# Score products of two heads: row halves instead of a stacked high and low part, in a one-layer encoder trunk

## The chip, the cores and the metric

The kernel runs on one core of one Trainium2 chip. The time is that of the device for one execution, in microseconds (us). An execution under the profiler gives the trace from which all rows below are taken; its busy times, waits and clocks belong to that one execution.

## The reference, cut to what matters

The input x has 2048 positions of 1024 values. One layer has two groups of attention heads beside each other, then an output projection, then a gated feed-forward block with a short convolution, and a last norm.

```
h = rmsnorm(x, attn_norm_g)
qa, ka, va, qb, kb, vb = split(h @ w_in, 6)          # 512 columns each
# group a: 8 heads of 64, each query chunk of 64 sees its own and the 8 chunks before it
scores = q k^T / 8 + relative bias;  o = softmax(scores) @ v
# group b: 4 heads, each with two score maps of width 64, all earlier chunks
w = softmax(q1 k1^T / 8 + bias) - lam * softmax(q2 k2^T / 8 + bias);  o = rmsnorm(w @ v)
x = x + concat(oa, ob) @ w_out
u = causal_dwconv(rmsnorm(x) @ w_up);  x = x + (silu(gate) * val) @ w_down
return rmsnorm(x)
```

What the change touches are the products q k^T of both groups. A score map contracts over 64 values. Two maps are always computed together: two heads of group a, or the two maps of one head of group b. The kernel calls them the two heads of a pair, and so does this text.

## The kernel before, in words

Each float32 operand of a product is held as two float16 parts, a high part and a low part (what the high part left over). A product is then three products: high by high, high by low, low by high (TERMS, line 64). The helper split (line 127) makes the parts: ScalarE writes the high part, then VectorE writes source minus high part as the low part.

The program has three stages. From 0 to 93 us x is normalised and transposed and the first projections run. From 93 to 1112 us the attention runs, in eight passes of one head pair each (ORDER, line 442). After that come the output projection, the feed-forward block and the last norm.

A pass holds 16 query blocks of 128 rows. For each, a front makes scores, biases and the softmax (front_a, line 464; front_b, line 526), and a back, two blocks later, multiplies by v (back_a, back_b). A front goes through pieces of 128 to 512 keys. For a piece it takes two score banks in PSUM, one a head, out of a pool of four (ps_s, line 210), calls scores, and lets VectorE add the bias and reduce the maximum (lines 484 and 543); only then is the bank free. Between the pieces stand the projections of the next pass as fill: proj_k makes the keys of 512 positions, proj_q the queries of 256. Their result stands in PSUM with head 0 on partitions 0 to 63 and head 1 on 64 to 127.

Before the change, proj_k splits each head by itself so that head 0's keys lie stacked in one slot, high part on partitions 0 to 63, low part on 64 to 127; head 1's lie the other way round in the second slot. proj_q also splits each head by itself, and two DMAs from ScalarE's queue then copy each head's high part to the other half of the partitions. So one product over 128 rows gives high query by high plus low key at once (line 438), and a product over 64 rows adds low query by high key (line 440).

The order of instructions on each engine is made when the program is built: a scheduler places them by a modelled time line, with the fronts, backs and splits at a raised priority. Each engine then executes its own list in that order and waits by semaphores.

Of the kernel before, what the change touches and what calls it, by code (L numbers as in the profile page):

```python
# [8 lines left out]
F16 = mybir.dt.float16  # L9
# [9 lines left out]
P = 128  # L19
# [29 lines left out]
QS = 2.0 ** -19  # L49
# [14 lines left out]
TERMS = ((0, 0), (0, 1), (1, 0))  # L64
# [3 lines left out]
def kernel(  # L68
# [18 lines left out]
    nc = tc.nc  # L87
# [39 lines left out]
    def split(hi, lo, src, scale):  # L127

        A.activation(hi, src, AF.Copy, scale=scale)  # L129
        V.scalar_tensor_tensor(lo, src, scale, hi, ALU.mult, ALU.subtract)  # L130
# [73 lines left out]
    with ExitStack() as at:  # L204
        kv = at.enter_context(tc.tile_pool(name="kv", bufs=8))
# [165 lines left out]
        def project(ps, hl, h, t0, t1, step):  # L371

            n = 0
            for c in range(NC):
                for a, b in TERMS:
                    nc.tensor.matmul(ps, lhsT=hl[:, a, c, :], rhs=h[:, b, c, t0:t1], start=n == 0, stop=n == 3 * NC - 1)  # L376
                    n += 1
                    if n % step == 0 and n < 3 * NC:
                        yield

        def proj_k(w, tg):

            ps = ps_mm.tile([P, TG], F32, name="mm")
            yield from project(ps, w["hl"][1], hT[tg], 0, TG, 6)
            ks = w["k"][tg] = kv.tile([P, 2, TG], F16, name="ks")
            with tc.high_priority(offset=HP):
                split(ks[0:64, 0], ks[64:128, 0], ps[0:64], QS)
                split(ks[64:128, 1], ks[0:64, 1], ps[64:128], QS)
            yield

        def proj_v(w, tg):
# [25 lines left out]
        def proj_q(w, k):  # L417


            i0 = w["halves"][k] * 2  # L420
            ps = ps_mm.tile([P, 2 * P], F32, name="mq", tag="mm")
            yield from project(ps, w["hl"][0], hT[i0 // 4], i0 % 4 * P, (i0 % 4 + 2) * P, 12)
            qs = w["q"][w["halves"][k]] = kv.tile([P, 2, 2, 2 * P], F16, name="qs", bufs=4)
            with tc.high_priority(offset=HP):
                for hd, (a, b) in enumerate(((0, 64), (64, 128))):
                    split(qs[a:b, hd, 0], qs[a:b, hd, 1], ps[a:b], QS)
            nc.scalar.dma_start(qs[64:128, 0, 0], qs[0:64, 0, 0])
            nc.scalar.dma_start(qs[0:64, 1, 0], qs[64:128, 1, 0])
            yield

        def scores(ps, w, i, k0, k1):


            g = k0 // TG
            ks, kc, qc = w["k"][g], slice(k0 - g * TG, k1 - g * TG), slice(i % 2 * P, (i % 2 + 1) * P)
            qs = w["q"][i // 2]
            for hd in range(2):
                nc.tensor.matmul(ps[hd], lhsT=qs[:, hd, 0, qc], rhs=ks[:, hd, kc], start=True, stop=False)  # L438
            for hd, (a, b) in enumerate(((0, 64), (64, 128))):
                nc.tensor.matmul(ps[hd], lhsT=qs[a:b, hd, 1, qc], rhs=ks[a:b, hd, kc], start=False, stop=True)  # L440

        ORDER = [4, 5, 0, 6, 1, 7, 2, 3]
        oTl = {}
# [20 lines left out]
        def front_a(w, i):  # L464
# [11 lines left out]
            for part, (a, b) in enumerate(((F, W), (0, F))):  # L476
                if a == b:
                    continue
                ps = [ps_s.tile([P, 512], F32, name="s") for hd in range(2)]
                for ka, kb in pieces(k0 + a, k0 + b, ()):  # L480
                    scores([p_[:, ka - k0 - a:kb - k0 - a] for p_ in ps], w, i, ka, kb)
                for hd in range(2):
                    bias = w["far"][:, hd, 384 - F:] if part else w["near"][:, hd, 256 - N:]
                    V.tensor_tensor_reduce(Sm[hd][:, a:b], ps[hd][:, :b - a], bias, 1.0, m[hd],
                                           ALU.add, ALU.max, mx[:, hd, part:part + 1])
                    m[hd] = mx[:, hd, part:part + 1]
                yield
# [38 lines left out]
        def front_b(w, i):  # L526
# [7 lines left out]
            for f, (a, b) in enumerate(reversed(pieces(0, W, (F,)))):  # L534
                ps = [ps_s.tile([P, 512], F32, name="s") for hd in range(2)]
                scores([p_[:, :b - a] for p_ in ps], w, i, a, b)
                for hd in range(2):
                    if a >= F:
                        bias = w["near"][:, hd, 256 - (W - a):256 - (W - b)]
                    else:  # L540
                        bias = w["near"][:, hd, 0:1].to_broadcast([P, b - a])
                    g, a0 = a // 1024, a % 1024
                    V.tensor_tensor_reduce(Sm[hd][g][:, a0:a0 + b - a], ps[hd][:, :b - a], bias, 1.0, m[hd],  # L543
                                           ALU.add, ALU.max, mx[:, hd, f:f + 1])
                    m[hd] = mx[:, hd, f:f + 1]
                yield
# [145 lines left out]
        def weights(n):  # L692

            p = ORDER[n]
            order = list(range(NT)) if p < 4 else [i for a in range(NT // 2) for i in (a, NT - 1 - a)]
            halves = []
            for i in order:
                if i // 2 not in halves:
                    halves.append(i // 2)
            return dict(p=p, order=order, halves=halves, hl={}, E={}, raw={}, k={}, v={}, q={}, P={}, o={}, ssq={})  # L700
# [5 lines left out]
        w = weights(0)  # L706
# [6 lines left out]
        for tg in range(NG):  # L713
            make_h(tg, xts if tg == 0 else None)
            if tg == 0:
                for k, j in enumerate((2, 1, 0)):
                    scan_w(w, ORDER[0], j, raws[k] if k < len(raws) else None)
                    load_w(w, j, (True, KF, Q1)[k])
            proj_v_first(w, tg)
            run(proj_k(w, tg))  # L720
            if tg == 0:
                run(proj_q(w, 0))
                make_lambda()
                make_profiles_b()
                load_bias(w, ORDER[0])
        run(proj_q(w, 1))
        make_profiles()

# [3 lines left out]
        def units(n):  # L732


            w = ws[n]
            q = [proj_q(w, k) for k in range(2, 8)]
            if n == NH2 - 1:
                kv_ = [[proj_k(w, g), proj_v(w, g)] for g in (2, 3)]
                return q[:2] + kv_[0] + q[2:4] + kv_[1] + q[4:]
            x = ws[n + 1]  # L740
            k, v = [proj_k(x, g) for g in range(NG)], [proj_v(x, g) for g in range(NG)]
            qx = [proj_q(x, 0), proj_q(x, 1)]
            if n == NH2 - 2:
                return q[:2] + [k[0]] + q[2:4] + [k[1], v[0]] + q[4:] + [v[1]] + qx
            return q[:2] + k[:2] + q[2:4] + k[2:] + q[4:] + v[:2] + qx + v[2:]
# [109 lines left out]
    with ExitStack() as fx:  # L855
# [250 lines left out]
        with tc.manual_schedule(engines={ET.PE, ET.DVE, ET.Activation, ET.Pool, ET.SP}):  # L1106
            prev, nq = None, Quarter(0, 0)
            for n, (b, pc) in enumerate(seq):
                if n == 3:
                    side[0] = nc.sync  # L1110
                q = nq
                scan = (n // 4 + 1, n % 4) if n // 4 + 1 < NK else None
                w = None if n < 2 or n // 2 + 1 >= NB else ups[n // 2 + 1]
# [99 lines left out]
    with ExitStack() as dx:  # L1213
# [36 lines left out]
        def down(q, k0, k1, scale):  # L1250

            ps = [ps_f.tile([P, TG], F32, name="mm") for _ in range(7)]

            ops = ((0, 0), (4, 6), (5, 4), (3, 3), (1, 5), (2, 1), (6, 2))
            last = k1 - (LASTK if q == NT // 2 - 1 else 1)
            g = {}
            order = [(kb, m) for kb in range(k0, last) for m in range(7)]
            order += [(kb, m) for ms in (range(5), range(5, 7)) for kb in range(last, k1) for m in ms]
            for kb, m in order:
                if kb not in g:  # L1260
                    g[kb] = load_g(q, kb, scale)
                go, wo_ = ops[m]
                for k, (a, c_) in enumerate(TERMS):
                    nc.tensor.matmul(ps[m].rearrange("p (c n) -> p c n", c=4), lhsT=g[kb][:, a, go],  # L1264
                                     rhs=wd[kb][:, :, c_, wo_],
                                     start=kb == k0 and k == 0, stop=kb == k1 - 1 and k == 2)
            return ps
# [19 lines left out]
        for q in range(NT // 2):  # L1287
            first = q == 0
            sc, iv = scales[-1]
            ps = down(q, 0, K1S if first else NK, sc)  # L1290
# [69 lines left out]
```

## Time and profile before

| what | us |
|---|---|
| median of 3 runs | 2537.67 (2528.0 to 2543.9) |
| the profiled execution | 2539.1 |
| its span | 2536.9 |
| TensorE busy in it (products) | 2377.2 (94%) |
| VectorE busy | 1890.7 (75%) |
| ScalarE busy | 1411.6 (56%) |
| GpSimd busy | 1170.2 (46%) |
| chain that ended last, TensorE's share | 48% of the span |

A busy time is a mean over stages. The chain of waits can be followed back to about 1117 us only, so the attention stage is read from the table by stage and from the waits of TensorE there. Durations of products overlap in the profile, as they are pipelined; what one costs in a stream is read from the distance between starts.

### The profile page before, as it was taken

The page shows a single profiled execution, that of the slowest core. Times are in us where ns is not written, and L with a number is a line of the kernel's source. Part 1 is how long each engine was busy: PE and PEld are TensorE (multiplying, and loading weights), DVE is VectorE, ACT ScalarE, POOL GpSimd, SP SyncE. Part 2 cuts the span into 40 slices and gives each one's busy share as a digit, 9 for nine tenths or more (in the row PEclk, how much of TensorE's full clock was granted, in tenths as well). Part 3 has the DMA queues.
Part 4 walks back from the last instruction along what each step waited for, and adds up shares of the span by engine and source line. Part 5 has one row for each costly group of instructions (what it writes and reads, how often), then busy time and mean ns, then how long its engine had stood idle before and what let it go on. Part 6 is the DMA issues. An engine that isn't in the chain of part 4 may idle for free.

```text
span 2536.9 us, 41286 instructions
## 1 busy us (share of the span) xinstructions
PE 2377.2 (94%) x14646; PEld 1209.7 (48%) x14646; DVE 1890.7 (75%) x4455; ACT 1411.6 (56%) x2495; POOL 1170.2 (46%) x1127
## 2 busy tenths in 40 slices
PE   5998989999999999899949999999999999999998
PEld 4655545555555555544414444444444444444443
DVE  6788988878877887856636888888887876656545
ACT  5565566656666667743345665666566553333322
POOL 2243344233433442222244656665666464766544
PEclk8998989999999999999969999999999999999999
DMA  7145446954695469998993243324333339323322
GB/s 213 38 81 94 96 92 107 168 104 80 115 162 108 90 112 208 208 228 255 269 227 107 95 129 105 125 94 128 105 121 97 113 107 408 105 88 113 108 88 79
DMA packets 636351, 340.60 MB, mean 134 GB/s; under 512 B 449944, under 2 KB 602832, under 8 KB 634736
## 3 DMA queue, kind: packets, MB, share of 16 engines
q1 hardware_dynamic: 615264, 316.15, 50.3%
q10 hardware_dynamic: 17712, 10.26, 1.6%
q0 software_dynamic: 3168, 11.56, 1.4%
q8 instruction: 114, 1.87, 0.3%
q14 instruction: 93, 0.76, 0.1%
HBM read 148.87 MB, written 85.21 MB: 92 GB/s over the span
## 4 chain that ended last, share of the span: by engine, by line
PE 48%; DMA 2%; POOL 2%; issue 1%; DVE 1%; ACT 1%; SPq 0%; ACTq 0%; DVEq 0%; POOLq 0%
PE mm L865 30%; PE mm L1264 13%; PE omm L660 5%; DMA wd<-gd 2%; SPq L1099 0%; POOL wuhl L983 0%; DMA wdraw<-in_w_down_dram 0%; DMA pt<-phl 0%; POOL Sx L974 0%; POOL wd L1241 0%; ACT wuraw L965 0%; DMA T<-td 0%; POOL wd L1242 0%; POOL wd L1244 0%; POOL wd L1243 0%
## 5 line engine op out<-in xcount | busy, mean ns | idle before, releaser
L865 PE MATMUL mm<-T,wuhl 128*128 128x512 f16 x3696 | 812.0, 382 | 43.8 <-ACT wuhl L985 28.4
L865 PEld LDWEIGHTS <-wuhl 128*128 128x128 f16 x3696 | 363.6, 99 | 484.5 <-ACT wuhl L985 29.9
L1264 PE MATMUL mm<-wd,ghl 128*128 128x512 f16 x1848 | 401.8, 380 | 2.9 <-ACT ghl L129 1.8
L376 PEld LDWEIGHTS <-whl 128*128 128x128 f16 x2976 | 274.8, 100 | 205.9 <-issue 36.6
L376 PE MATMUL mm<-h,whl 128*128 128x512 f16 x1440 | 354.4, 389 | 2.9 <-DVE qs L130 2.5
L1264 PEld LDWEIGHTS <-ghl 128*128 128x128 f16 x1848 | 180.7, 98 | 223.3 <-ACT ghl L129 2.9
L569 POOL TENSOR_TENSOR phl<-St,phl 128x1024 f16<-128x1024 f32 (+7 forms) x96 | 157.6, 1652 | 229.1 <-ACT phl L568 169.6
L1064 DVE SCALAR_TENSOR_TENSOR Y<-U,taps,Y 128x1024 f32<-128x1024 f32 x176 | 256.6, 1458 | 1.6
L438 PE MATMUL s<-ks,qs 128*128 128x128 f16 (+3 forms) x720 | 194.4, 297 | 42.9 <-DVE mxb L543 22.6
L129 ACT ACTIVATE ghl<-wd,gsc 128x384 f16<-128x384 f32 (+1 forms) x176 | 106.7, 660 | 196.1 <-DMA wd<-gd 97.1
L550 ACT ACTIVATE St<-St,nb,sc 128x1024 f32<-128x1024 f32 (+4 forms) x192 | 187.9, 980 | 42.2 <-DVE nb L547 42.0
L130 DVE SCALAR_TENSOR_TENSOR ghl<-wd,gsc,ghl 128x384 f16<-128x384 f32 (+1 forms) x176 | 135.7, 805 | 95.6 <-ACT ghl L129 95.0
L376 PE MATMUL mq<-h,whl 128*128 128x256 f16 x1536 | 202.2, 278 | 3.9 <-DVE qs L130 3.4
L543 DVE CUSTOM_DVE_ANT_0 St<-s,near,mxb 128x512 f32<-128x512 f32 (+3 forms) x280 | 169.3, 621 | 20.9 <-PE s L440 16.6
L494 POOL TENSOR_TENSOR phl<-St,phl 128x640 f16<-128x640 f32 (+2 forms) x64 | 82.1, 1284 | 222.1 <-ACT phl L493 202.8
L440 PE MATMUL s<-ks,qs 64*128 64x128 f16 (+3 forms) x720 | 177.8, 301 | 0.0
L660 PE MATMUL omm<-wohl,oT 128*128 128x512 f16 x672 | 154.0, 382 | 1.4 <-DVE wohl L130 1.4
L1068 ACT ACTIVATE Y<-Y 128x1024 f32<-128x1024 f32 x44 | 46.5, 1057 | 191.1 <-DVE Y L1064 191.1
L974 POOL TENSOR_TENSOR Sx<-wuraw 128x512 f32<-128x512 f32 x44 | 78.5, 1785 | 158.4 <-ACT wuraw L965 151.2
L895 DVE SCALAR_TENSOR_TENSOR wdhl<-wdraw,wd_sc,wdhl 128x128 f16<-128x128 f32 x132 | 128.8, 996 | 14.2 <-ACT wdhl L892 13.8
L440 PEld LDWEIGHTS <-qs 64*128 64x128 f16 x720 | 54.6, 93 | 169.2 <-issue 155.0
L492 ACT ACTIVATE St<-St,nb,sc 128x640 f32<-128x640 f32 (+4 forms) x128 | 107.9, 843 | 39.2 <-DVE nb L489 38.2
(228 smaller groups left out, 3974.5 us busy)
## 6 DMA issues: line engine op xcount, KB each, us to landing
wd<-gd SPq DMA_DIRECT2D x88, 256.0 KB, 2.8
wuraw<-in_w_up_dram SPq DMA_DIRECT2D x42, 512.0 KB, 5.0
gd<-Y SPq DMA_DIRECT2D x42, 512.0 KB, 3.2
wdraw<-in_w_down_dram SPq DMA_DIRECT2D x154, 128.0 KB, 2.7
wd<-wdd SPq DMA_DIRECT2D x11, 1792.0 KB, 12.7
wdd<-wdhl SPq DMA_DIRECT2D x41, 448.0 KB, 2.7
wraw<-in_w_in_dram SPq DMA_DIRECT2D x24, 512.0 KB, 4.6
td<-hl SPq DMA_DIRECT2D x24, 512.0 KB, 4.5
```

The costliest lines, as they stand in the source:

```text
L130: V.scalar_tensor_tensor(lo, src, scale, hi, ALU.mult, ALU.subtract)
L376: nc.tensor.matmul(ps, lhsT=hl[:, a, c, :], rhs=h[:, b, c, t0:t1], start=n == 0, stop=n == 3 * NC - 1)
L438: nc.tensor.matmul(ps[hd], lhsT=qs[:, hd, 0, qc], rhs=ks[:, hd, kc], start=True, stop=False)
L440: nc.tensor.matmul(ps[hd], lhsT=qs[a:b, hd, 1, qc], rhs=ks[a:b, hd, kc], start=False, stop=True)
L543: V.tensor_tensor_reduce(Sm[hd][g][:, a0:a0 + b - a], ps[hd][:, :b - a], bias, 1.0, m[hd], ALU.add, ALU.max, mx[:, hd, f:f + 1])
L550: A.activation(Sm[hd][g], Sm[hd][g], AF.Exp, bias=nb[:, hd:hd + 1], scale=w["sc"], accum_out=l[:, hd, g:g + 1])
L569: nc.gpsimd.tensor_tensor(hl[:, 1], Sm[0][g], hl[:, 0], ALU.subtract)
L660: nc.tensor.matmul(ps[n], lhsT=oc[:, a], rhs=wo[ORDER[c]][:, b, n * TG:(n + 1) * TG], start=k == 0, stop=k == 3 * NC - 1)
L865: nc.tensor.matmul(ps, lhsT=hl[:, a, wop, c * P:(c + 1) * P], rhs=Tt[:, b, c, :], start=start and k == 0, stop=k == 11, skip_group_check=n ...
L895: V.scalar_tensor_tensor(dst, src, scale, h, ALU.mult, ALU.subtract)
L1064: V.scalar_tensor_tensor(Y, self.U[j][:, tap:D + tap], self.u.taps[j][:, tap:tap + 1], Y, ALU.mult, ALU.add)
L1264: nc.tensor.matmul(ps[m].rearrange("p (c n) -> p c n", c=4), lhsT=g[kb][:, a, go], rhs=wd[kb][:, :, c_, wo_], start=kb == k0 and k == 0, s ...
```

## The change

The keys of both heads are split in one step, and so are the queries: slot 0 holds the high parts of both heads on their own partition halves, slot 1 the low parts. The copies by DMA go. The scores of a piece become six products over 64 rows each: three terms, and in each term head 0 on the lower half of the rows and head 1 on the upper half.

```diff
@@ proj_k
             with tc.high_priority(offset=HP):
-                split(ks[0:64, 0], ks[64:128, 0], ps[0:64], QS)
-                split(ks[64:128, 1], ks[0:64, 1], ps[64:128], QS)
+                split(ks[:, 0], ks[:, 1], ps, QS)
@@ proj_q
-            qs = w["q"][w["halves"][k]] = kv.tile([P, 2, 2, 2 * P], F16, name="qs", bufs=4)
+            qs = w["q"][w["halves"][k]] = kv.tile([P, 2, 2 * P], F16, name="qs", bufs=4)
             with tc.high_priority(offset=HP):
-                for hd, (a, b) in enumerate(((0, 64), (64, 128))):
-                    split(qs[a:b, hd, 0], qs[a:b, hd, 1], ps[a:b], QS)
-            nc.scalar.dma_start(qs[64:128, 0, 0], qs[0:64, 0, 0])
-            nc.scalar.dma_start(qs[0:64, 1, 0], qs[64:128, 1, 0])
+                split(qs[:, 0], qs[:, 1], ps, QS)
@@ scores
-            for hd in range(2):
-                nc.tensor.matmul(ps[hd], lhsT=qs[:, hd, 0, qc], rhs=ks[:, hd, kc], start=True, stop=False)
-            for hd, (a, b) in enumerate(((0, 64), (64, 128))):
-                nc.tensor.matmul(ps[hd], lhsT=qs[a:b, hd, 1, qc], rhs=ks[a:b, hd, kc], start=False, stop=True)
+            for n, (qa, ka) in enumerate(TERMS):
+                for hd, (a, b) in enumerate(((0, 64), (64, 128))):
+                    nc.tensor.matmul(ps[hd], lhsT=qs[a:b, qa, qc], rhs=ks[a:b, ka, kc], start=n == 0, stop=n == 2)
```

The scheduler makes a new order from it. On TensorE, a piece of 512 keys in the middle of a pass of group b stood like this before (s_7884 is head 0's bank, s_7885 head 1's; L438 is the product over 128 rows, L440 over 64; mm is a projection):

```order
L438 LDWEIGHTS qs_7342
L438 MATMUL s_7884<-ks_5373,qs_7342 128x512
L440 LDWEIGHTS qs_7342
L440 MATMUL s_7884<-ks_5373,qs_7342 128x512
L376 LDWEIGHTS whl_7027
L376 MATMUL mm_7978<-h_568,whl_7027 128x512
L438 LDWEIGHTS qs_7342
L438 MATMUL s_7885<-ks_5373,qs_7342 128x512
L440 LDWEIGHTS qs_7342
L440 MATMUL s_7885<-ks_5373,qs_7342 128x512
```

The same piece now (s_8060 and s_8061 are the banks, L435 the products over 64 rows):

```order
L435 LDWEIGHTS qs_7504
L435 MATMUL s_8060<-ks_5481,qs_7504 128x512
L435 LDWEIGHTS qs_7504
L435 MATMUL s_8061<-ks_5481,qs_7504 128x512
L435 LDWEIGHTS qs_7504
L435 MATMUL s_8060<-ks_5481,qs_7504 128x512
L435 LDWEIGHTS qs_7504
L435 MATMUL s_8061<-ks_5481,qs_7504 128x512
L435 LDWEIGHTS qs_7504
L435 MATMUL s_8060<-ks_5481,qs_7504 128x512
L435 LDWEIGHTS qs_7504
L435 MATMUL s_8061<-ks_5481,qs_7504 128x512
```

Here the two heads alternate and no other work stands between them. A piece of 256 keys in a later block, now, stands otherwise; before, its two heads were parted by one projection product, as in the first piece above:

```order
L435 LDWEIGHTS qs_7898
L435 MATMUL s_8554<-ks_5564,qs_7898 128x256
L435 LDWEIGHTS qs_7898
L435 MATMUL s_8554<-ks_5564,qs_7898 128x256
L435 LDWEIGHTS qs_7898
L435 MATMUL s_8554<-ks_5564,qs_7898 128x256
L376 LDWEIGHTS whl_7179
L376 MATMUL mm_8503<-h_823,whl_7179 128x512
L435 LDWEIGHTS qs_7898
L435 MATMUL s_8555<-ks_5564,qs_7898 128x256
L435 LDWEIGHTS qs_7898
L435 MATMUL s_8555<-ks_5564,qs_7898 128x256
```

All three products of head 0 come first, then a projection product, then those of head 1.

On ScalarE, around one query tile of a pass of group a, before (L129 is split's step on ScalarE, L427 the copy; L493 and L357 belong to a softmax and to the bias):

```order
L129 ACTIVATE qs_5978<-mq_5919 64x256
L492 ACTIVATE St_6013,l_6009<-St_6013,nb_6010,sc_4216 128x640
L492 ACTIVATE St_6014,l_6009<-St_6014,nb_6010,sc_4216 128x640
L493 ACTIVATE phl_5872<-St_5874 128x640
L493 ACTIVATE phl_5872<-St_5875 128x640
L357 ACTIVATE near_5952<-near_5952,isc_5950 128x512
L427 DMA qs_5978<-qs_5978 64x256
L338 ACTIVATE whl_5790<-wraw_5788 128x1024
L129 ACTIVATE qs_5978<-mq_5919 64x256
```

The same tile now:

```order
L443 ACTIVATE ohl_6176<-osb_5807 128x512
L129 ACTIVATE ks_5974<-mm_5870 128x512
L142 ACTIVATE whl_6560,ws_ss_6561<-wraw_6558,gam_78 128x1024
L129 ACTIVATE qs_6102<-mq_6041 128x256
L357 ACTIVATE near_6074<-near_6074,isc_6072 128x512
L338 ACTIVATE whl_5906<-wraw_5904 128x1024
L129 ACTIVATE qs_6194<-mq_6105 128x256
```

One step where two and a copy stood, and the neighbours are others.

One more place of TensorE's order before is needed to read the trace: a run of four products over 64 rows, of two pieces (512 and 256 columns), at 802 us. Head 0's banks are s_10771 and s_10739, head 1's s_10772 and s_10740.

```order
L440 LDWEIGHTS qs_10358
L440 MATMUL s_10771<-ks_9223,qs_10358 128x512
L440 LDWEIGHTS qs_10358
L440 MATMUL s_10739<-ks_9326,qs_10358 128x256
L440 LDWEIGHTS qs_10358
L440 MATMUL s_10772<-ks_9223,qs_10358 128x512
L440 LDWEIGHTS qs_10358
L440 MATMUL s_10740<-ks_9326,qs_10358 128x256
```

Both of head 0 stand ahead of both of head 1.

## Rows read from the trace of the kernel before

**Rows 1.** Busy time by stage: length, then PE, PEld, DVE, ACT, POOL (instructions), clock, DMA.

```profile
core 0: us, PE busy (x) PEld busy (x) DVE busy (x) ACT busy (x) POOL busy (x), PEclk, DMA share, GB/s
93.00:1112.00 1019.00, 952.56 (x7748) 542.97 (x7745) 829.42 (x2558) 661.36 (x1338) 357.34 (x217) 0.96 0.65 122
1300.00:2537.00 1237.00, 1208.40 (x5574) 547.54 (x5574) 888.81 (x1414) 617.07 (x960) 729.29 (x843) 0.99 0.38 124
```

**Rows 2.** TensorE's waits, 93 to 1112 us: total us, times, longest.

```profile
PE s L438 <- DVE mxb L543: 22.6, 29, 2.6
PE s L438 <- DVE mx L484: 15.5, 19, 1.5
...
PE mq L376 <- DVE qs L130: 3.4, 2, 2.9
...
PE s L438 <- DMA qs<-qs: 2.4, 1, 2.4
```

**Rows 3.** TensorE in order of time: start, length, product, count, idle before.

```profile
617.84 0.38 PE L438 MATMUL s<-ks,qs 128*128 128x512 f16 x1 [1.16 <-DVE mxb L543]
618.15 0.39 PE L440 MATMUL s<-ks,qs 64*128 64x512 f16 x1
618.47 0.61 PE L376 MATMUL mq<-h,whl 128*128 128x256 f16 x4
```

**Rows 4.** The same view in the feed-forward stage.

```profile
1360.85 36.42 PE L865 MATMUL mm<-T,wuhl 128*128 128x512 f16 x168
...
1397.25 36.42 PE L865 MATMUL mm<-T,wuhl 128*128 128x512 f16 x168
```

**Rows 5.** The same view at the run of four; rows merge, the first shape shows.

```profile
802.06 0.59 PE L438 MATMUL s<-ks,qs 128*128 128x512 f16 x2
802.59 0.50 PE L440 MATMUL s<-ks,qs 64*128 64x512 f16 x4
803.02 0.50 PE L376 MATMUL mq<-h,whl 128*128 128x256 f16 x3
```

**Rows 6.** Groups by line: count, busy us, mean ns, idle before and its releasers.

```profile
L130 DVE SCALAR_TENSOR_TENSOR qs<-mq,qs 64x256 f16<-64x256 f32 x128 | 53.5, 418 | 6.5 <-ACT qs L129 4.2
...
L129 ACT ACTIVATE qs<-mq 64x256 f16<-64x256 f32 x128 | 48.1, 376 | 66.9 <-DVE qs L130 42.5 <-PE s L440 11.0 <-PE mq L376 10.4
...
L130 DVE SCALAR_TENSOR_TENSOR ks<-mm,ks 64x512 f16<-64x512 f32 x64 | 44.1, 688 | 9.9 <-ACT ks L129 8.0
...
L129 ACT ACTIVATE ks<-mm 64x512 f16<-64x512 f32 x64 | 37.8, 591 | 28.3 <-DVE ks L130 13.3 <-PE mm L376 13.3 <-PE s L440 0.5
...
L130 DVE SCALAR_TENSOR_TENSOR vt<-mm,vt 128x512 f16<-128x512 f32 x28 | 19.1, 682 | 0.6 <-ACT vt L129 0.4
```

**Rows 7.** ScalarE's waits, 93 to 1112 us.

```profile
ACT qs L129 <- DVE qs L130: 42.5, 21, 5.6
...
ACT ks L129 <- DVE ks L130: 12.4, 10, 4.0
```

**Rows 8.** Busy time and clock in two stretches that follow each other.

```profile
205.00:210.40 5.40, 2.57 (x12) 0.79 (x10) 4.48 (x12) 2.82 (x6) 3.23 (x2) 1.00 0.47 114
210.50:213.80 3.30, 3.30 (x10) 1.14 (x8) 3.30 (x13) 0.17 (x1) 0.00 (x0) 0.50 1.02 188
```

**Rows 9.** The query tile's copies on ScalarE's queue: count, ns min/median/max.

```profile
L427 ACTq DMA_DIRECT2D qs<-qs x64: 467/468/1077, 54.7 to 1071.2; - x64
L428 ACTq DMA_DIRECT2D qs<-qs x64: 467/468/554, 58.1 to 1074.7; - x64
```

**Rows 10.** VectorE in order of time around 621 us.

```profile
620.71 2.00 DVE L118 TENSOR_SCALAR rs_y<-rs_y 128x4 int32<-128x4 int32 x1
622.62 0.73 DVE L543 CUSTOM_DVE_ANT_0 St<-s,near,mxb 128x512 f32<-128x512 f32 x1
```

## The prediction

> **What bounds the kernel now.** I read the table by stage first [rows 1]. The attention stage, from the first score product at 93 us to the last at 1112 us, is 1019 us long. TensorE is busy for 952.6 us of it, VectorE for 829.4 (81%), ScalarE for 661.4 (65%). So TensorE sets the pace there, and 66.4 us of the stage are its idle time. The mean granted clock is 0.96, so 0.04 x 1019 = 41 us of full-speed work are lost to stretches at the lower level. The feed-forward stage that follows keeps TensorE busy for 1208 of 1237 us, and the last 6,175 products of the program stand in the same order in both kernels: I take it as unmoved.
>
> Then the waits of TensorE in the attention stage [rows 2]: 22.6 + 15.5 = 38.1 us, in 48 waits, are score products that wait until VectorE has emptied a score bank; 3.4 us are a query projection that waits for a bank held by a split; 2.4 us are one wait for a copied query. VectorE is late because of its queue: a tiny step of 128x4 holds it for 2.00 us [rows 10], and the reductions behind it, and so the score product, come late. The stretches at a clock of 0.50 follow such idle time [rows 8]: TensorE was busy for 2.57 of 5.4 us, and the next 3.3 us ran at half speed (1.2 instead of 2.4 GHz).
>
> **The score products.** First the price of a switch [rows 3]. Products over all 128 rows that follow each other are 36.40 us / 168 = 0.217 us apart at 512 columns [rows 4], which is 0.423 ns a column. From a 128-row score product to a 64-row one it is 618.15 - 617.84 = 0.31 us, and from there to a 128-row product 0.32 us. So going in costs 0.093 us and coming out 0.103 us, 0.2 us for each excursion into 64-row products, whatever its length.
>
> Two 64-row products on different halves run side by side. More is seen in the run of four [rows 5]. It is the four 64-row products of the last piece of order in the section on the change: first half 512 and 256 columns, second half 512 and 256, in this order. They take 803.02 - 802.59 = 0.43 us until the next product. The longer half alone is 768 x 0.423 = 0.325 us, and with the way out 0.428 us. So the halves run beside each other even where two products of one half stand before those of the other, and the weights of the second product of a half were loaded under the first. For such a follow-up I take 10 ns, the resolution of the rows; the bounds are 0 and the 0.093 us of an entry, where the weight load has no cover.
>
> The counts come from the program's order in both kernels. Before: 720 128-row products with 210,944 columns; 720 64-row products in 582 excursions (453 of one product, 121 of two), whose longer halves sum to 176,128 columns. Together 387,072 x 0.423 ns = 163.7 us, and 582 x 0.2 = 116.4 us: 280.1 us. After: 2,160 64-row products in 408 excursions; longer halves 429,824 columns, 181.8 us; 408 x 0.2 = 81.6 us; 1,035 follow-ups x 10 ns = 10.4 us: 273.8 us. So the change does not save a third of the score time: the old second products were mostly alone, but the new ones often are as well (148 excursions hold the three products of one head only). **Term 1: -6 us** (with follow-ups at 0: -17; with all at 0.093: +80; the new form has no row of its own, but its follow-ups are nearest to rows 5).
>
> The Trainium skill says otherwise on order (TensorE: Matmul & The Clock Gate, Part 3: Packing small matmuls — row/col tiling): matmuls start and end strictly in program order. By that the four products of [rows 5] would have taken 0.217 + 0.217 + 0.108 + 0.103 = 0.645 us, against 0.43 us in the trace, so the trace disagrees.
>
> **The splits.** A split is one ScalarE and one VectorE instruction. The page's groups show that time goes by columns, not partitions: 64x512 takes 688 ns on VectorE and 128x512 takes 682 [rows 6]. So each removed half saves its whole time. VectorE: 64 x 418 ns + 32 x 688 ns = 26.8 + 22.0 = 48.8 us. ScalarE: 64 x 376 + 32 x 591 ns = 24.1 + 18.9 = 43.0 us. ScalarE also loses 42.5 + 12.4 us of waiting, in which the second half's first step stood behind VectorE [rows 7], and 128 issues of the query copies at 0.468 us in its queue [rows 9], though many lie under a running instruction. The copies' transfers, 32 KB each, were not late except once (the 2.4 us). None of this is on TensorE's path by itself: it counts as far as it shortens the waits for late banks.
>
> How far, I estimate. VectorE's idle time in the stage rises from 190 to about 238 us (a factor of 0.80 on how crowded it is), ScalarE's from 358 to 401 (0.89); together 0.71. I take a quarter off the 38.1 us, 9.5 us, and the 2.4 us of the query copy: **term 2: -12 us**. The bounds are none of it, since the new order of VectorE's queue can put other work ahead of the reductions, and all of the 38.1 + 3.4 + 2.4 = 44 us. As the low clock follows idle time, I scale its 41 us with that: 12 / 66.4 x 41 = **term 3: -7 us** (bounds 0 and 44 / 66.4 x 41 = -27). The query tile of half the size frees memory that nothing waits for, and I cost it at nothing. Before 93 us four key splits and two query splits are shortened, at most 3 us, which I leave in the range.
>
> **The sum.** The profiled execution took 2539.1 us, 2.2 us beside its span of 2536.9, and stands 1.4 us above the median of the runs (2537.67). 2539.1 - 6 - 12 - 7 = 2514 us.
>
> **The rivals.**
> *Only the products change.* VectorE's order is new in most places, and waits set by order can move instead of going. Then term 1 alone remains: 2533 us. For it: 81% is not a full engine, and the long hold in [rows 10] is an instruction that the change does not touch. Chance 0.26.
>
> *Nearly all waits for late banks go*: -6 - 44 - 27, 2462 us. Against it: the hold in [rows 10], which stays. Chance 0.08.
>
> *Long score runs find no banks.* This ends slower. There are four score banks. No excursion before is longer than four products; after, 61 hold twelve or more, and 47 of these touch all four banks with no other work between, so TensorE comes to the second piece sooner and waits there with everything behind it. If each of the 61 brings one more wait of the present mean, 38.1 / 48 = 0.79 us, that is 48 us, and with the clock (times 41 / 66.4) 30 us more: 2533 + 78 = 2611 us; with half of them, 2572 us. It decides from about 24 such waits on (24 x 0.79 x 1.62 = 31 us), where the 2533 us of the next-to-likeliest case have grown past the median by 1%. For it: the score products wait for VectorE already. Against it: VectorE is relieved, and where a run comes late the banks are empty. Chance 0.12.
>
> *Weights are not loaded under the product of the same half.* Then 1,035 follow-ups cost 0.093 us: +80 us, 2619 us. The run of four [rows 5] speaks against it, where it would have made 0.43 into 0.52 us. Chance 0.03. That is a rule of the Trainium skill (same page and part): a weight load overlaps running matmuls only where the row group is another one. The trace disagrees [rows 5].
>
> *The halves keep program order in long runs.* Then the columns after are 465,920 and term 1 is +9 (197.1 + 81.6 + 10.4 - 280.1): 2548 us if no wait goes. Against it, again: [rows 5]. Chance 0.04.
>
> The forecast has 0.47. Its own range runs from 2476 (three quarters of the bank waits with their clock, 33 + 20 us, and follow-ups at 5 ns) to 2533. The range 2476 to 2552 takes in the case of 2533 us, that of 2548 us and the mildest tenth of the long runs; it leaves out 0.08 below and about 0.13 above.
>
> A measurement of this kernel tells about 1% (25 us) from no change, so faster means under 2512 us. My forecast lies just at this edge; as its bounds reach further down than up, I put 0.28 of its 0.47 below, and with the 0.08: faster 0.36. Same: 0.19 + 0.26 + 0.04 + 0.01 of the mildest long runs = 0.50. Slower: 0.11 + 0.03 = 0.14.
>
> **What would show it.** Right: score products in one run of three pairs at 512 columns take about 0.87 us from the first to the next other product (0.093 + 3 x 0.217 + 2 x 0.01 + 0.103); VectorE about 49 and ScalarE 43 us less busy, no query copies in ScalarE's queue; waits for the reductions near 29 us and the clock at 0.97 in the stage. Wrong: follow-ups of 0.3 us at 512 columns (weights not covered); waits for the reductions above 38 us, at the long runs; a feed-forward stage that has moved, since I say it has not; or a gain above 60 us, which would mean that ScalarE's or VectorE's queue set the pace more than TensorE's busy time tells.

## The result, and the profile after

The changed kernel took 2552.55 us in the median of 10 runs (2546.82 to 2558.93), the kernel before 2537.19 us (10 runs). The ratio is 1.0064, 95% interval 1.0052 to 1.0076. It is 0.6% slower; I had forecast 0.9% faster, and the time lies 0.55 us beyond the range. The profiled execution took 2548.26 us, 9.2 us above that of before.

The loss is in the attention stage. From the first score product to the last back product it is 1050.7 us instead of 1038.9, and it begins 2.7 us later. By the first product of the feed-forward stage the program is 15.0 us behind, of which 5 are won back in the first up-projections.

By stage, columns as in [rows 1] (first the attention from first to last score product, 1032.6 us against 1019):

```profile
95.70:1128.30 1032.60, 952.94 (x8478) 554.04 (x8477) 763.72 (x2469) 611.75 (x1249) 357.33 (x218) 0.95 0.60 116
1310.00:2546.00 1236.00, 1207.54 (x5580) 546.84 (x5578) 900.91 (x1414) 619.64 (x964) 735.77 (x844) 0.99 0.38 124
```

VectorE is busy 66 us less in the stage and ScalarE 50 us less, yet the stage is longer. TensorE's busy time is what it was (952.9 us, before 952.6), so nearly all of the added time is idle time of TensorE: 79.7 us instead of 66.4. Its waits, as in [rows 2]:

```profile
PE s L435 <- DVE mxb L538: 27.0, 22, 5.9
PE s L435 <- DVE mx L479: 22.4, 23, 2.9
PE o L584 <- DMA pt<-phl: 12.6, 12, 2.1
PE o L510 <- DVE osb L514: 8.1, 7, 2.3
PE o L510 <- DMA pt<-phl: 6.6, 6, 2.8
```

The waits of the backs before, which [rows 2] does not show (L589 and L515 are the backs' products):

```profile
PE o L515 <- DMA pt<-phl: 4.5, 3, 2.6
PE o L589 <- DMA pt<-phl: 3.5, 4, 1.6
...
PE o L515 <- DVE osb L519: 1.2, 2, 0.7
```

Score products wait 49.4 us for VectorE's reductions instead of 38.1. Backs wait 19.2 us for transposed weights instead of 8.0, and 8.1 us for their output bank instead of 1.2. The stretches at half clock, taken from the trace's record of the granted clock, sum to 99 us from the first score product to the last back product; before it was 75.

The products themselves came out cheaper than I had taken them. Two places in TensorE's order, start and length as in [rows 3]; the first is a run of two pieces of 512 columns, the second has the three products of one head at 256 columns:

```profile
601.27 1.47 PE L435 MATMUL s<-ks,qs 64*128 64x512 f16 x12
602.67 0.50 PE L376 MATMUL mq<-h,whl 128*128 128x256 f16 x3
...
598.22 0.50 PE L435 MATMUL s<-ks,qs 64*128 64x256 f16 x3
598.65 0.39 PE L376 MATMUL mq<-h,whl 128*128 128x256 f16 x2
```

Twelve products take 1.40 us = 6 x 0.217 + 0.10, so the pairs run side by side and a follow-up costs nothing that these rows show. The three products of one head take 0.43 us = 3 x 0.108 + 0.10: nothing beside them, and nothing for loading weights under them. The Trainium skill (TensorE: Matmul & The Clock Gate, Part 3: Packing small matmuls — row/col tiling) says in one place that a weight load overlaps running products only in another row group. These three are of one group, so the trace disagrees, as it did before the change [rows 5]. The same part of the Trainium skill also lets a load into a background weight buffer go ahead of running products; these rows would fit that.

The splits became what was forecast, columns as in [rows 6]:

```profile
L130 DVE SCALAR_TENSOR_TENSOR qs<-mq,qs 128x256 f16<-128x256 f32 x64 | 26.4, 412 | 6.1 <-ACT qs L129 6.0
L129 ACT ACTIVATE qs<-mq 128x256 f16<-128x256 f32 x64 | 23.8, 371 | 23.3 <-PE mq L376 23.3
L130 DVE SCALAR_TENSOR_TENSOR ks<-mm,ks 128x512 f16<-128x512 f32 x32 | 21.9, 685 | 21.6 <-ACT ks L129 21.6
L129 ACT ACTIVATE ks<-mm 128x512 f16<-128x512 f32 x32 | 18.6, 581 | 8.3 <-PE mm L376 8.2
```

The waits of ScalarE for VectorE between the halves [rows 7] are gone; it waits for the products instead.

### The profile page after: what moved, and what is told of

Read it like the earlier page. It is cut to its first block, busy times and chain, and to the rows that moved or that the text cites. A ratio compares the mean times of both kernels' runs of the same rounds, so it can differ in the third digit from the quotient of the medians.

```text
span 2546.5 us, 42262 instructions
## 1 busy us (share of the span) xinstructions
PE 2375.8 (93%) x15366; PEld 1220.3 (48%) x15366; DVE 1835.1 (72%) x4359; ACT 1356.9 (53%) x2399; POOL 1173.7 (46%) x1127
## 3 DMA queue, kind: packets, MB, share of 16 engines
q1 hardware_dynamic: 615264, 316.15, 49.4%
## 4 chain that ended last, share of the span: by engine, by line
PE 43%; DVE 5%; DMA 3%; POOL 3%; issue 3%; ACT 2%; SPq 1%; DVEq 0%; POOLq 0%; ACTq 0%
PE mm L860 22%; PE mm L1259 14%; PE omm L655 6%; DVE Y L1059 1%; DMA wd<-gd 1%; DVE wdhl L890 1%; POOL wuhl L978 1%; ACT wuraw L960 1%; DMA wdraw<-in_w_down_dram 1%; DMA pt<-phl 1%; SPq L1094 0%; ACT wdhl L887 0%; ACT Y L1063 0%; POOL Sx L969 0%; PE o L510 0%
## 5 line engine op out<-in xcount | busy, mean ns | idle before, releaser
L860 PE MATMUL mm<-T,wuhl 128*128 128x512 f16 x3696 | 811.0, 382 | 41.6 <-ACT wuhl L980 27.7
L435 PE MATMUL s<-ks,qs 64*128 64x256 f16 (+3 forms) x2160 | 278.1, 296 | 51.0 <-DVE mxb L538 27.0
L564 POOL TENSOR_TENSOR phl<-St,phl 128x1024 f16<-128x1024 f32 (+7 forms) x96 | 162.7, 1705 | 242.8 <-ACT phl L563 215.2
L376 PE MATMUL mq<-h,whl 128*128 128x256 f16 x1536 | 211.1, 285 | 0.0
L129 ACT ACTIVATE ghl<-wd,gsc 128x384 f16<-128x384 f32 (+1 forms) x176 | 106.7, 661 | 195.7 <-DMA wd<-gd 95.2
L435 PEld LDWEIGHTS <-qs 64*128 64x128 f16 x2160 | 113.8, 96 | 175.1 <-issue 132.4
L538 DVE CUSTOM_DVE_ANT_0 St<-s,near,mxb 128x512 f32<-128x512 f32 (+2 forms) x280 | 166.8, 621 | 20.7 <-PE s L435 17.4
L890 DVE SCALAR_TENSOR_TENSOR wdhl<-wdraw,wd_sc,wdhl 128x128 f16<-128x128 f32 x132 | 138.4, 1066 | 24.1 <-ACT wdhl L887 23.2
L563 ACT ACTIVATE phl<-St 128x1024 f16<-128x1024 f32 (+7 forms) x96 | 75.6, 803 | 107.6 <-DMA pt<-phl 74.2
```

Source lines behind the costliest of these rows:

```text
L435: nc.tensor.matmul(ps[hd], lhsT=qs[a:b, qa, qc], rhs=ks[a:b, ka, kc], start=n == 0, stop=n == 2)
L564: nc.gpsimd.tensor_tensor(hl[:, 1], Sm[0][g], hl[:, 0], ALU.subtract)
L860: nc.tensor.matmul(ps, lhsT=hl[:, a, wop, c * P:(c + 1) * P], rhs=Tt[:, b, c, :], start=start and k == 0, stop=k == 11, skip_group_check=n ...
L890: V.scalar_tensor_tensor(dst, src, scale, h, ALU.mult, ALU.subtract)
```

## The experiments

All ratios are to the kernel before, timed beside the variant. Five theories were set against each other. A: product time on TensorE, by columns and excursions, sets the pace. B: products over 64 rows are dear by themselves, wherever they stand. C: any new order moves the time by chance. L: what counts is how early the first head's score bank is complete, in the order in which the products are written. H: the softmax loop through two buffers sets the pace.

**One tile for both banks, kernel before and after.**

```diff
-                ps = [ps_s.tile([P, 512], F32, name="s") for hd in range(2)]
+                pair = ps_s.tile([P, 2, 512], F32, name="s")
+                ps = [pair[:, hd] for hd in range(2)]
```

(and two such tiles in the pool instead of four banks.)

> The kernel before, with the two score banks of a piece taken as one tile of two banks, so that both heads become free together and their four products stand together in the order (360 excursions into 64-row products instead of 582; halves 108,800 columns instead of 176,128). Theory A (score products cost what their columns and excursions cost, and waits for banks are added to that): product time 207 us instead of 280, so up to -73 us; as a bank is now given back only when both heads are reduced, waits may grow by up to 40 us: 2465 to 2505 us. Theory B (products over 64 rows are dear by themselves, how they stand matters little): within 10 us of 2537. Theory C (any new order moves the time by 10 to 20 us either way, no trend): 2520 to 2555.

> The changed kernel with the same tile of two banks (355 excursions instead of 408; halves 335,360 columns instead of 429,824). Theory A: product time 213 us instead of 263, so up to -50 us against the changed kernel, and within 15 us of the kernel before with the same tile, since their product times are 213 and 207 us and the splits are cheaper here: 2465 to 2515 us. Theory B (64-row products are dear by themselves, by a lower clock or otherwise): 20 us or more slower than the kernel before with the same tile. Theory C: no trend, 2535 to 2570.

Before with the pair: 2543.96 us, ratio 1.0026 (1.0010 to 1.0041). After with it: 2555.10 us, 1.0062 (1.0043 to 1.0081). Theory A, which had allowed 40 us for banks that are given back in pairs, falls here; theories B and C allow the time before. The stage of the kernel before with paired banks, and its waits:

```profile
98.10:1118.30 1020.20, 887.10 (x7727) 530.76 (x7724) 821.21 (x2561) 661.63 (x1340) 354.30 (x218) 0.95 0.63 122
```

```profile
PE s L438 <- DVE mxb L545: 43.0, 41, 4.5
PE s L438 <- DVE mx L485: 23.0, 25, 3.8
PE o L591 <- DMA pt<-phl: 13.9, 15, 2.2
```

TensorE's busy time fell by 65 us, close to the 73 us of the count, and all of it came back as idle time: the stage is 1020 us as it was. The run changes two things at once, though, cheaper products and banks that come free only in pairs, so it does not show what the saving alone would be worth. The after kernel is slower than the before kernel by 0.4% even where their product times are alike. That is less than theory B's 20 us, so B falls too.

**The two products of a head written together, kernel before.** For each head the product over 128 rows, then that over 64, instead of both of the first kind and then both of the second.

```diff
-            for hd in range(2):
-                nc.tensor.matmul(ps[hd], lhsT=qs[:, hd, 0, qc], ...
-            for hd, (a, b) in enumerate(((0, 64), (64, 128))):
+            for hd, (a, b) in enumerate(((0, 64), (64, 128))):
+                nc.tensor.matmul(ps[hd], lhsT=qs[:, hd, 0, qc], ...
                 nc.tensor.matmul(ps[hd], lhsT=qs[a:b, hd, 1, qc], ...
```

> The kernel before, with the same four products written head by head (128-row then 64-row product of head 0, then of head 1); nothing else. The order has 702 excursions instead of 582, halves 209,408 columns instead of 176,128. Theory A: product time 318 us instead of 280, 20 to 45 us slower, 2557 to 2582 us. Theory C (an order is luck): anywhere within 20 us of 2537.

2528.90 us, ratio 0.9957 (0.9943 to 0.9971): the fastest kernel of the study, with the dearest products. Its stage and first waits:

```profile
95.30:1108.80 1013.50, 973.66 (x7750) 557.00 (x7746) 824.39 (x2562) 663.85 (x1341) 358.83 (x218) 0.97 0.64 123
```

```profile
PE s L438 <- DVE mx L483: 11.5, 10, 2.3
PE o L514 <- DMA pt<-phl: 10.2, 3, 5.5
PE s L438 <- DVE mxb L542: 9.4, 16, 1.6
```

TensorE is busy 21 us longer than before, its waits at score products are 20.9 us instead of 38.1, and the clock is 0.97. The half-clock time is 55 us instead of 75. Against theory A again, which had it 20 to 45 us slower; theory C allowed it.

**The six products written head by head, kernel after.**

```diff
-            for n, (qa, ka) in enumerate(TERMS):
-                for hd, (a, b) in enumerate(((0, 64), (64, 128))):
+            for hd, (a, b) in enumerate(((0, 64), (64, 128))):
+                for n, (qa, ka) in enumerate(TERMS):
```

> The changed kernel with its six products written head by head: three of head 0, then three of head 1; nothing else. Product time by columns and excursions 269 us against 263. Theory L (what counts is when a head's bank is complete: written pair by pair, both heads are complete only with the last pair, and VectorE's reductions start late and together): 8 to 20 us faster than the changed kernel, 2532 to 2545 us. Theory A, by now weak (product time on TensorE sets the pace): 5 us slower, 2552 to 2560. Theory H (the stage is paced by the softmax loop through two buffers and the transposing transfers): within 6 us of 2552.

2532.91 us, ratio 0.9984 (0.9969 to 1.0000): 20 us faster than the changed kernel (by the two ratios) with the same instructions. Theory L allows it, theories A and H do not. Its waits at score products, and a run of six that stands in the program as three of head 0, then three of head 1:

```profile
PE s L435 <- DVE mxb L538: 14.0, 11, 3.1
...
PE s L435 <- DVE mx L479: 11.4, 11, 2.8
```

```profile
508.69 0.83 PE L435 MATMUL s<-ks,qs 64*128 64x512 f16 x6
509.45 0.39 PE L376 MATMUL mq<-h,whl 128*128 128x256 f16 x2
```

The six take 0.76 us, about 3 x 0.217 + 0.10, and their single records start in twos, 0.010 us apart. So on the chip the two heads run side by side here too and are complete together, although they are written one behind the other. The same kernel timed again, one execution:

> A second look at the kernel written head by head: 2527 to 2542 us, as before.

2539.92 us beside a median of 2539.22 for the kernel before. That lies in the range, but does not show the lead of 6 us again; executions of this kernel had spread over 15 us. Two more orders give the dose, one with head 0 complete at the fourth product and one as the change has it but with the heads swapped:

```diff
-            for n, (qa, ka) in enumerate(TERMS):
-                for hd, (a, b) in enumerate(((0, 64), (64, 128))):
+            for hd, n in ((0, 0), (1, 0), (0, 1), (0, 2), (1, 1), (1, 2)):   # fourth, rows and terms from hd and n
+            for hd, n in ((1, 0), (0, 0), (1, 1), (0, 1), (1, 2), (0, 2)):   # swapped, another kernel
```

> The changed kernel with its six products written so that head 0 is complete with the fourth (head 0, head 1, head 0, head 0, head 1, head 1); with the third it was 2533 us, with the fifth, as the change has it, 2553. Theory L (the earlier the first head's bank is complete as written, the better): between the two, 2533 to 2548 us. Theory C (luck of an order): anywhere from 2525 to 2575, and not between them in particular.

> The changed kernel with the heads of each pair of products written the other way round, head 1 first; the first complete bank still comes with the fifth product, but is head 1's, while VectorE's reductions are written head 0 first. Theory L: no better than the changed kernel, 2548 to 2565 us. Theory C: an equivalent order falls elsewhere, outside 2545 to 2560.

Fourth: 2543.43 us, 1.0024 (1.0011 to 1.0037). Swapped: 2556.92 us, 1.0072 (1.0056 to 1.0089). So the ratio climbs 0.9984, 1.0024, 1.0064, with the first head complete at the third, fourth and fifth product, and the swap is no better than the fifth. Theory L forecast each of these three times; theory C allowed the fourth as well and missed the swap.

**The same in the kernel before, the other way.** Its two products over 64 rows swapped, so that head 0, which VectorE reduces first, is complete last:

```diff
-            for hd, (a, b) in enumerate(((0, 64), (64, 128))):
+            for hd, a, b in ((1, 64, 128), (0, 0, 64)):
                 nc.tensor.matmul(ps[hd], lhsT=qs[a:b, hd, 1, qc], ...
```

> The kernel before with its two 64-row products of a piece written head 1 first, so that head 0's bank, which VectorE reduces first, is complete with the fourth product instead of the third; head 1's with the third. The same instructions, 585 excursions against 582. Theory L: 5 to 15 us slower than the kernel before, 2543 to 2553 us. Theory C (luck): anywhere from 2520 to 2560, not above 2543 in particular.

2546.30 us, 1.0033 (1.0016 to 1.0050): as theory L forecast, though its waits for the reductions are only 42.1 us in its profile (38.1 before); here the half-clock time rose more, to 92 us from 75.

**The splits apart again**, with the new products, written by pairs and by heads, and once with the two copies put back into a third slot that nobody reads.

```diff
-                split(ks[:, 0], ks[:, 1], ps, QS)
+                for a, b in ((0, 64), (64, 128)):
+                    split(ks[a:b, 0], ks[a:b, 1], ps[a:b], QS)
-                split(qs[:, 0], qs[:, 1], ps, QS)
+                for a, b in ((0, 64), (64, 128)):
+                    split(qs[a:b, 0], qs[a:b, 1], ps[a:b], QS)
...
+            nc.scalar.dma_start(qs[64:128, 2], qs[0:64, 0])    # the copies, in the last of the three alone
+            nc.scalar.dma_start(qs[0:64, 2], qs[64:128, 0])
```

> The changed kernel, but each head's half of a key or query split as its own step, as before the change (64 more steps of 376 and 418 ns and 32 more of 591 and 688 ns on ScalarE and VectorE); no copies, new products. If the saved split time shortens the waits for score banks (my prediction's second term): 10 to 25 us slower than the changed kernel, 2562 to 2578 us. If the splits hide beside TensorE's work: within 6 us of it plus 10 us for its dearer order (product time 274 us instead of 263): 2550 to 2568 us.

> Written head by head as in the kernel of 2533 us, but with each head's half of a key or query split as its own step. If the merged splits are worth the 12 us seen with the pairs: 2545 us, 2538 to 2552. If they are worth nothing once the banks are complete early: within 5 us of 2533. What is then left above the kernel before (2538) is the price of the new products alone.

> The kernel with new products, pair by pair, and each head's split by itself (2565 us), with the two copies of the queries' high parts put back, into a slot that nobody reads. If the copies' issues in ScalarE's queue cost: 5 to 15 us slower, 2570 to 2580 us. If they hide: within 6 us of 2565.

By pairs: 2564.76 us, 1.0099 (1.0074 to 1.0123). By heads: 2547.24 us, 1.0028 (1.0014 to 1.0042). With copies: 2560.32 us, 1.0081 (1.0054 to 1.0108). The merged splits are worth 0.35% with the pairs and 0.44% by heads, 9 to 11 us of the 49 and 43 us that they take off VectorE and ScalarE. The intervals leave 2 to 16 us for the first and 6 to 17 us for the second, and by pairs both stated ranges held the result, so that run did not decide between them. The copies hide. The table has the ratios; its rows are the operations, its columns the way the products are written.

| | term by term, heads in turn | head by head |
|---|---|---|
| kernel before | 1 | 0.9957 |
| new products, halves split apart | 1.0099 | 1.0028 |
| new products, merged splits (the change) | 1.0064 | 0.9984 |

**More buffers.** Three instead of two for the softmax weights' parts (with the larger query tile of the kernel before, the buffers do not fit), with the products by pairs and by heads:

```diff
-                hl = sb.tile([P, 2, n], F16, name="phl", tag="HL", bufs=2)
+                hl = sb.tile([P, 2, n], F16, name="phl", tag="HL", bufs=3)   # and the tag's other tiles
```

> The changed kernel with three buffers instead of two for the high and low parts of the weights (tag HL), which the smaller query tile makes room for; nothing else. ScalarE waits 103 us in the changed kernel for a transposing transfer to free one of these buffers, 73 us in the kernel before. Theory H: most of these waits go, 15 to 40 us faster than the changed kernel, 2512 to 2537 us. Theory L or a limit elsewhere: within 8 us of 2552.

> The changed kernel written head by head (2533 us) and with three HL buffers (2537 us with the pairs): if the two gains of 20 and 15 us are of different waits: 2518 us, 2510 to 2525, faster than the kernel before. If both shorten the same thing, the time that a score bank is held: 2525 to 2537 us.

By pairs: 2537.39 us, 0.9981 (0.9968 to 0.9994), 15 us faster than the changed kernel, within 0.4 us of theory H's range and not as theory L had it; by heads: 2542.75 us, 1.0017 (1.0001 to 1.0034), 10 us slower than without the third buffer, which neither expectation allowed. The gains do not add, theory H fails head by head, and what an order does by chance (theory C) may be of this size too.

**Five score banks instead of four** (two for projections instead of three), and **score products pinned** behind all that is written ahead of them:

```diff
-MB = 3
+MB = 2
...
+                    tc.keep_in_program_order(
-                    nc.tensor.matmul(ps[hd], lhsT=qs[a:b, qa, qc], ...
+                        nc.tensor.matmul(ps[hd], lhsT=qs[a:b, qa, qc], ...))   # in another kernel
```

> The changed kernel with five score banks and two banks for projections instead of four and three. If score products wait because four banks are too few for their longer runs (49 us of waits at score products in the changed kernel, 38 before): 10 to 25 us faster than the changed kernel, 2527 to 2542. If the waits only show that VectorE is late by its own queue: within 8 us of 2552, or slower by up to 20 us where projections lack banks.

> The changed kernel, with each score product kept behind all products written ahead of it in the program, so that projections and backs stand between the pieces as written (396 excursions instead of 408, halves 360,832 columns instead of 429,824, product time 232 us instead of 263). Theory A: 20 us or more faster, below 2532. Theory C (order moves waits more than product time): within 20 us of 2552 either way. Theory L: no faster, as the pairs end together as in the changed kernel, 2550 to 2570.

2580.37 us (1.0167) and 2759.78 us (1.0862): both outside every range, theory L's for the pins among them. With five banks the score products wait less, 27.7 us, but projections (mm) and row sums (am) now wait for VectorE, which I take for waits for one of their two banks:

```profile
PE mm L376 <- DVE nsc L348: 11.3, 2, 5.6
PE am L148 <- DVE ks L130: 10.9, 6, 4.0
```

With pins, backs wait 127.2 us for transposed weights, as nothing may pass them (22 waits, up to 13.7 us). The scheduler's freedom is worth far more here than the 31 us of product time by which the pinned order is cheaper by the count.

## Why the prediction was wrong

*"So TensorE sets the pace there."* This premise failed, and with it term 1 as a term of the sum. The products did become cheaper, by more than I said: with follow-ups at nothing the count is 263 us against 280, the -17 us end of my bounds. It did not shorten the stage: TensorE's busy time stayed, as more of it ran at half clock, and its idle time grew by 13 us. The paired banks (73 us cheaper by the count, 0.26% slower) and the kernel before written head by head (38 us dearer, 0.43% faster) both show the time going another way than the product time. A TensorE that is 93% busy in a stage need not be the bound: its busy time holds the switches between row layouts (116 us by the count before), which in the paired kernel were partly replaced by waits. I read its busy share as the pace, though the page warns that this engine's busy time is modelled.

*Term 2, -12 us for the splits.* Its size was about right: 9 to 11 us by the two comparisons in the table, with the split times within 2% of the rows. That is luck in part. It was a guess, a quarter off the waits, between bounds of 0 and 44 us, and it holds in time, not in the waits that I hung it on: I had the waits for the reductions fall to about 29 us, and they grew to 49.4. Above 38 us was one of my own signs of being wrong.

*Term 3, -7 us for the clock.* That half clock follows idle time holds for all but one stretch of the changed kernel; the sign failed with the waits: half-clock time went from 75 to 99 us, about 12 us more lost.

*What was not in the sum* is the price of the new form, 18 us written head by head (1.0028 - 0.9957; the copies that also go hide), and about as much again for writing it term by term (20 us against head by head; the kernel before, written in the like manner, pays 11 for it). Together with the 11 us that the merged splits give back, this is the measured +16: -11 + 18 - 11 + 20. Both prices may be the same kind of thing: how long a score bank is held. Pairing the order's products and reductions with the trace, I took for each of the 648 banks the time from its first product to the end of its reduction: 4.01 us in the mean before and 4.13 after. The fill, first product to the end of the last (its start plus 0.423 ns a column), rose from 0.49 to 0.67 us, since a head needs three products of its own half and has a neighbour beside it less often than the count of pairs suggests; the reduction came 0.07 us sooner. Nine kernels fall nearly in line: 3.48 (0.9957), 3.70 (0.9984), 3.80 (three buffers, 0.9981), 3.88 (fourth, 1.0024), 3.99 (1.0028), 4.07 (swapped, 1.0072), 4.12 (copies, 1.0081), 4.13 (1.0064), 4.30 us (1.0099). The kernel before (4.01, 1), the same with its 64-row products swapped (4.02, 1.0033), the third buffer by heads (3.79, 1.0017), the paired banks (4.09, 1.0026, and 3.91, 1.0062) and five banks (5.40, 1.0167) lie off it, and the pinned kernel has the shortest hold of all (2.86 us) and is the slowest. Each mean is of one execution; the head-by-head kernel had 3.70 in one and 3.81 in another. That the hold is the cause is argued from this line, not shown.

The traces also speak against theory L as a mechanism on the chip. In the mean of the 324 pieces, head 0's bank was complete 0.61 us after the piece's first product when written head by head, 0.69 us with the fourth and 0.67 us with the fifth, which is no dose; but its reduction began after 3.11, 3.28 and 3.58 us. So what the written order moved was VectorE's lateness, from the full bank to the start of its reduction (2.5 to 3.1 us in the nine kernels), and this hangs on VectorE's order, which the scheduler makes anew from each way of writing. Theory L forecast the times; that the written order acts through the scheduler's choices is the reading that fits the traces, and no run here separates it.

*The rivals.* The one that ended on the other side, long score runs without banks, named the right place: score products wait longer for banks. This is the longest wait behind another score product, in a run of nine:

```profile
624.14 0.82 PE L435 MATMUL s<-ks,qs 64*128 64x512 f16 x6
628.52 0.48 PE L435 MATMUL s<-ks,qs 64*128 64x256 f16 x3 [3.56 <-DVE mxb L538]
```

The waits for reductions behind another score product went from 20.9 us in 30 to 30.6 in 30, most of the rise but not the 48 us of that rival. The 61 runs of twelve or more hold 15.9 us of them, in 19 waits. Head by head there are 64 such runs, with 8.7 us in 11, and the waits in all are half. So long runs take part, but do not make the loss by themselves. The rival on weights is excluded by the two places shown in the result, the one on program order by the six products written head by head, and the feed-forward stage did not move.

## What to carry to other kernels

Before a saving on the busiest engine is counted, ask what it does next: where its waits are for a few buffers that other engines empty, a cheaper product can be paid back as waiting. Look then at how long each buffer is held, from the first write to the last read; here time went with that in many kernels, not in all. Two heads that share an engine were better written one behind the other, in both forms (11 and 20 us), though with this scheduler and for a reason that is not shown. And where a scheduler orders the program, the same instructions written in another order can be worth more than the change itself (here 20 us against 15): compare each form in its own best order.

## What the runs showed of the hardware

The clock fell after a stretch in which TensorE was never idle. From 528.4 to 533.7 us of the changed kernel it did one 64-row product of 512 columns at a time, on one half of its rows, in turn with a back product of 64 columns; the next 6.8 us ran at 0.50 (1.2 instead of 2.4 GHz):

```profile
528.40:533.70 5.30, 5.30 (x26) 2.16 (x23) 2.55 (x8) 0.00 (x0) 0.00 (x0) 1.00 0.06 12
534.00:540.80 6.80, 6.80 (x31) 2.83 (x28) 2.88 (x12) 4.60 (x8) 0.00 (x0) 0.50 0.18 33
```

```profile
528.41 0.39 PE L435 MATMUL s<-ks,qs 64*128 64x512 f16 x1
528.73 0.20 PE L510 MATMUL o<-vs,pt 128*128 128x64 f16 x1
528.86 0.39 PE L435 MATMUL s<-ks,qs 64*128 64x512 f16 x1
529.18 0.20 PE L510 MATMUL o<-vs,pt 128*128 128x64 f16 x1
```

Each such turn takes 0.45 us, of which 0.2 are the switches. The head-by-head kernel did the like ahead of two of its stretches, from 516.1 and 717.5 us, with no idle time either. All other stretches at half clock in the attention stages of the kernel before and the changed one have idle time of TensorE shortly ahead, 1.2 us or more in sum over 5 us; what makes the clock fall is not worked out here.

Products on different row halves overtake each other within a run, by [rows 5] (0.43 us for four) and by the six written head by head (0.76 us): two or three products of one half do not hold up the other half's that stand behind them.
